# FFN up products as seven block products of eight, on one Trainium2 core

## The chip, the core and the metric

The kernel runs on one core of a Trainium2 chip. Five engines work beside each other, each through its own queue in order: TensorE (PE, matmuls into PSUM; PEld is its weight load), VectorE (DVE), ScalarE (ACT), GpSimd (POOL) and SyncE (SP), which issues the DMAs. The metric is the device time of one execution in microseconds. Less is better.

## The reference

Two layers over 512 latent tokens (x) and 256 context tokens (ctx) of width 1024. Each layer is a half-step SwiGLU FFN, a token mixer (a convolution, gated linear attention and attention beside each other), and a second half-step FFN; each of them is preceded by an RMS norm with a scale, shift and gate that come from a conditioning vector, one set for x and one for ctx.

```python
def pre(x, mod, j, g):
    return rms_norm(x, g) * (1 + mod[:, :, 3 * j + 1]) + mod[:, :, 3 * j]

def half_ffn(x, mod, j, g, w1, w2):
    gu = pre(x, mod, j, g) @ w1
    a, u = jnp.split(gu, 2, axis=-1)
    return x + 0.5 * mod[:, :, 3 * j + 2] * ((jax.nn.silu(a) * u) @ w2)
...
    for i in range(DEPTH):
        mod_x = (sc @ w_ada[i] + b_ada[i]).reshape(B, 1, N_MOD, D)
        mod_c = (scc @ w_ada[i] + b_ada[i]).reshape(1, 1, N_MOD, D)
        x, ctx = layer(x, ctx, mod_x, mod_c, ...)
    return x
```

w1 is 1024 x 5632 (gate and up, 22 tiles of 128 columns each), w2 is 2816 x 1024. In the last FFN only x is needed, so it works on 512 tokens instead of 768.

## The kernel before, in words

Activations lie transposed: 128 channels on the partitions, the 768 tokens along the row (x first), eight K tiles for the width of 1024 (KT = 8). Every product of float32 values is made of three passes: an operand is split into a rounded part and the rest (`split`, lines 141 to 143: a copy on ScalarE, a subtraction on VectorE), and `mm3` (386 to 393) multiplies hi by hi, lo by hi and hi by lo into one PSUM sum. The weights go the same way: `load_split` (132 to 139) loads a tile of 128 x 1024, two load buffers deep, and splits it into `whi` and `wlo`, three deep.

There are four FFNs (two per layer), here called FFN 1 to 4, with a mixer between 1 and 2 and between 3 and 4. `ffn` (402) goes over 22 hidden tiles f. `up` (413) makes the gate tile and the up tile of f: for each of the eight K tiles three passes over two column ranges, 386 and 384 columns (256 and 258 in FFN 4). The columns are the tokens and two more that hold the shifts. The activation that goes in is x times the scale only (class `Scale`, 336): 1 / rms per token comes in when the sum leaves PSUM, in `evac` (462, lines 465 and 468), so products can start before the norm is known. Then silu(gate) times up is split (`gh`, `gl`). `down` (485) multiplies two hidden tiles at a time by w2: for each of eight output tiles d and each of the segments (512 columns of x, 256 of ctx) two times three matmuls, and `add_gated` (line 399, VectorE) adds the sum times the gate onto the residual `xt`. The products of a pair of hidden tiles follow one pair later.

The modulation vectors (w_ada, 1024 x 9216 per layer) are made beside the FFNs: `ada` (183) loads 128 x 512 pieces, ScalarE multiplies them by the conditioning value, once for x and once for ctx (line 195), VectorE adds them up (line 197), and a matmul with a matrix of ones (206) sums over the partitions. `fill` advances them a few steps per hidden tile, so they are spread over the FFN. The first two vectors are made on TensorE at the start (`ada_first`, 211).

`Stats` (247) sums the squares of the finished residual tiles (ScalarE squares, GpSimd adds at line 263), and gets 1 / rms with thirteen small VectorE steps (line 282 and `rsqrt`, 145).

The mixer (`mix`, 518) is a long chain of smaller products. The order of instructions on each engine is set by a planner that weighs costs and due times, with TensorE's order by hand (`tc.manual_schedule`) only in the first products (`up_head`, 429) and in the attention loop. GpSimd has no work in the FFNs but the sums of squares at their ends.

## Time and profile before

| | us |
|---|---|
| median of 3 timed runs | 2857.68 (2856.6 to 2858.29) |
| span of the profiled execution | 2857.3 |
| PE busy | 2781.7 (97%) |
| PEld busy | 2541.2 (89%) |
| DVE busy | 1768.5 (62%) |
| ACT busy | 1200.8 (42%) |
| POOL busy | 136.4 (5%) |

The profiled execution's own time is its span from the first to the last instruction, 2857.3 us; it lies between the timed runs. Busy time of an engine is the time in which at least one of its instructions runs. Matmuls overlap their neighbours by their drain, so the listed duration of one is longer than the step from its start to the next start. A stretch of the span is given as start:end in us; PEclk is the granted TensorE clock as a share of 2.4 GHz.

### The profile page before, as it was taken

Reading aid. Unit: us, or ns where it says so; the run is one execution under the profiler, and the core shown is the slowest. Engines: PE = TensorE matmul, PEld = TensorE weight load, DVE = VectorE, ACT = ScalarE, POOL = GpSimd, SP = SyncE. Lnnn points to the kernel's source line nnn. Section 1 sums busy time; section 2 is a strip of 40 time slices with the busy share of each in tenths; the row PEclk is TensorE's granted clock in tenths of the full one; section 3 lists DMA queues with packets and bytes.
Section 4 is the critical chain, followed back from the end, with each engine's and each line's share of the span. In section 5 each row is a group of like instructions: output and inputs, shape, how many; then the busy total and the mean of one; then the engine's idle time right before and its main releaser. Section 6 shows DMA issues by size and latency. Waiting matters only on the chain. (4 is left out here: it accounts for less than half of the span.)

```text
span 2857.3 us, 42932 instructions
## 1 busy us (share of the span) xinstructions
PE 2781.7 (97%) x17498; PEld 2541.2 (89%) x17498; DVE 1768.5 (62%) x2974; ACT 1200.8 (42%) x1908; POOL 136.4 (5%) x134
## 2 busy tenths in 40 slices
PE   8999999999899999999999999999999989999999
PEld 4999999988687899999999999999997768999998
DVE  4786874464897565566465746454546588555555
ACT  4665662233347454254252523232324447432322
POOL 1000000010300100000000100000001110100000
PEclk9999999999999999999999999999999999999999
DMA  7443441221211243233231313231312131222322
GB/s 255 144 144 129 141 130 60 67 93 58 65 43 27 86 139 101 82 118 107 78 118 56 116 66 111 74 119 60 98 57 84 47 88 28 91 89 95 98 97 89
DMA packets 98501, 267.67 MB, mean 94 GB/s; under 512 B 11520, under 2 KB 11904, under 8 KB 98304
## 3 DMA queue, kind: packets, MB, share of 16 engines
q1 hardware_dynamic: 98304, 264.93, 28.7%
q8 instruction: 137, 2.24, 0.3%
q14 instruction: 60, 0.49, 0.1%
HBM read 249.16 MB, written 7.34 MB: 90 GB/s over the span
## 5 line engine op out<-in xcount | busy, mean ns | idle before, releaser
L137 ACT CAST whi<-raw 128x1024 fp32r<-128x1024 f32 (+1 forms) x314 | 324.6, 1044 | 1110.8 <-PE up L391 524.2
L389 PE MATMUL up<-sh,whi 128*128 128x386 f32 (+1 forms) x2808 | 691.4, 327 | 2.2 <-ACT sh L362 1.2
L391 PE MATMUL up<-sl,whi 128*128 128x386 f32 (+1 forms) x2808 | 687.8, 325 | 4.7 <-DVE sl L363 4.7
L393 PE MATMUL up<-sh,wlo 128*128 128x386 f32 (+1 forms) x2808 | 686.0, 325 | 0.1
L465 DVE TENSOR_TENSOR upv<-up,rb 128x770 f32<-128x770 f32 (+2 forms) x177 | 157.2, 889 | 639.0 <-PE up L393 634.7
L389 PEld LDWEIGHTS up<-sh,whi 128*128 128x128 f32 x2808 | 493.1, 190 | 12.4 <-ACT whi L137 4.2
L391 PEld LDWEIGHTS up<-sl,whi 128*128 128x128 f32 x2808 | 495.9, 190 | 7.5 <-DVE sl L363 7.3
L393 PEld LDWEIGHTS up<-sh,wlo 128*128 128x128 f32 x2808 | 494.1, 190 | 2.1 <-DVE upv L465 1.7
L399 DVE SCALAR_TENSOR_TENSOR xt<-dn,mods,xt 128x512 f32<-128x512 f32 (+1 forms) x616 | 375.2, 632 | 123.0 <-PE dn L393 122.3
L389 PE MATMUL dn<-gh,whi 128*128 128x512 f32 (+1 forms) x1232 | 429.9, 349 | 3.3 <-DVE xt L399 3.2
L138 DVE TENSOR_TENSOR wlo<-raw,whi 128x1024 fp32r<-128x1024 f32 (+1 forms) x314 | 378.6, 1215 | 83.3 <-ACT whi L137 75.1
L391 PE MATMUL dn<-gl,whi 128*128 128x512 f32 (+1 forms) x1232 | 427.7, 347 | 0.0
L393 PE MATMUL dn<-gh,wlo 128*128 128x512 f32 (+1 forms) x1232 | 426.4, 347 | 0.0
L195 ACT ACTIVATE adat<-adaw,sc 128x512 f32<-128x512 f32 x392 | 258.9, 715 | 84.0 <-DVE adacc L197 76.7
L389 PEld LDWEIGHTS dn<-gh,whi 128*128 128x128 f32 x1232 | 232.8, 189 | 45.0 <-ACT whi L137 7.9
L393 PEld LDWEIGHTS dn<-gh,wlo 128*128 128x128 f32 x1232 | 232.9, 189 | 31.2
L391 PEld LDWEIGHTS dn<-gl,whi 128*128 128x128 f32 x1232 | 233.0, 189 | 29.5
L197 DVE TENSOR_TENSOR adacc<-adacc,adat 128x512 f32<-128x512 f32 x392 | 250.4, 684 | 7.9 <-ACT adat L195 6.3
L468 ACT ACTIVATE upv<-upv 128x512 f32<-128x512 f32 (+1 forms) x308 | 179.7, 625 | 33.8 <-DVE upv L465 33.6
L389 PE MATMUL pj<-nh,whi 128*128 128x512 f32 (+1 forms) x328 | 120.5, 371 | 8.5 <-DVE var L572 4.3
L263 POOL TENSOR_TENSOR acc<-acc,sq 128x512 f32<-128x512 f32 (+1 forms) x72 | 76.1, 1057 | 1075.1 <-ACT sq L260 1069.7
L391 PE MATMUL pj<-nl,whi 128*128 128x512 f32 (+1 forms) x328 | 120.9, 369 | 2.4 <-DVE nl L332 2.3
(216 smaller groups left out, 2798.7 us busy)
## 6 DMA issues: line engine op xcount, KB each, us to landing
raw<-in_w_dram SPq DMA_DIRECT2D x264, 512.0 KB, 3.5
adaw<-in_wada_dram SPq DMA_DIRECT2D x288, 256.0 KB, 3.3
raw<-in_wt_dram SPq DMA_DIRECT2D x26, 512.0 KB, 3.4
raw<-in_wo_dram SPq DMA_DIRECT2D x16, 512.0 KB, 3.6
raw<-in_wk_dram SPq DMA_DIRECT2D x8, 416.0 KB, 3.2
xt<-in_xT_dram SPq DMA_DIRECT2D x8, 384.0 KB, 7.9
park<-xt SPq DMA_DIRECT2D x8, 384.0 KB, 2.3
xt<-park SPq DMA_DIRECT2D x8, 384.0 KB, 5.2
```

The source lines that it names most:

```text
L137: nc.scalar.copy(out=hi[:, :n], in_=r[:, :n])
L138: nc.vector.tensor_tensor(out=lo[:, :n], in0=r[:, :n], in1=hi[:, :n].bitcast(F32), op=ALU.subtract)
L195: nc.scalar.activation(out=t, in_=r, func=AF.Copy, scale=sc[:, k, v:v + 1])
L197: nc.vector.tensor_tensor(out=acc[v], in0=acc[v], in1=t, op=ALU.add)
L263: eng.tensor_tensor(out=self.acc[:, t0:t0 + n], in0=self.acc[:, t0:t0 + n], in1=s[:, :n], op=ALU.add)
L389: nc.tensor.matmul(out=o, lhsT=w[0], rhs=m[0][:, t0:t0 + n], start=first, stop=False)
L391: nc.tensor.matmul(out=o, lhsT=w[0], rhs=m[1][:, t0:t0 + n], start=False, stop=False)
L393: nc.tensor.matmul(out=o, lhsT=w[1], rhs=m[0][:, t0:t0 + n], start=False, stop=last)
L399: nc.vector.scalar_tensor_tensor(out=x, in0=o[:, :n], scalar=mods[l][:, v, mod * KT + d:mod * KT + d + 1], in1=x, op0=ALU.mult, op1=ALU.add)
L465: nc.vector.tensor_tensor(out=a[:, t0:t0 + n], in0=p[:, c0:c0 + n], in1=rb[:, t0:t0 + n], op=ALU.mult)
L468: nc.scalar.activation(out=a[:, c], in_=a[:, c], func=AF.Silu if t == f else AF.Identity, bias=a[:, NX + v:NX + v + 1])
```

## The change

The up product of an FFN is a 2 x 2 x 2 block product: the tokens are cut into two halves h (384 each, 256 in FFN 4; half 0 is all x), K into two halves of four K tiles, and the output into gate and up. The Winograd form of Strassen's scheme makes it with seven block products and sums of blocks. In the code they are named by the activation operand: 11 and 21 (half 0, K half 0 and 1), 22 (half 1, K half 1) and T1 to T4 (differences of normalised blocks). Each product is four K tiles times three passes. Partial results are shared: `up` adds products onto PSUM data that ScalarE or VectorE has written (`b` is a copy of `a`, `c` is a sum of `a` and `z`), after one dummy matmul per bank. Four PSUM banks a, b, c, d change roles from one hidden tile to the next.

Since differences of normalised values are needed, the norm is applied before the products (class `Combos` in place of `Scale`): normalise half 0 and split it, then normalise half 1, form the differences (VectorE and GpSimd) and split them. For the first four hidden tiles of an FFN (HEADS) the products 11 and 21, which need half 0 only, come first, while half 1 is being built; their results are kept in SBUF.

The weight operands are sums too: a class `Feed` loads weight tiles (five load buffers), lets GpSimd form the sums of 128 x 512 blocks (four for each hidden tile), and splits them into units of 512 columns, in a ring of seven. A unit is refilled when the product after the one that used it has been issued (`release`). Down products use units of 512 as well, and the last four hidden tiles' down products are made together in `tail`. The mixers' weight tiles become two units each.

In `ffn` all engines' queues now follow the program order (`tc.manual_schedule()` without a list of engines). The modulation vectors advance by `tick`, after each block product and each down tile; per piece VectorE does the product and sum for x in one instruction, ScalarE the product for ctx and GpSimd the sum for ctx. The sum over partitions takes one-column matmuls.

Also changed: the output projection and the last down products of FFN 2 are cut 384 + 384 instead of 512 + 256; the sines and cosines are loaded per mixer.

The diff, cut to its core:

```diff
+HEADS = 4
+RAW = 5
+RING = 7
...
-    def load_split(src, n=1024):
-        r = wp.tile([P, 1024], F32, tag="raw", name="raw", bufs=2)
+    def load(src, n=1024):
+        r = wp.tile([P, 1024], F32, tag="raw", name="raw", bufs=RAW)
         nc.sync.dma_start(out=r[:, :n], in_=src)
-        hi = wp.tile([P, 1024], F32R, tag="whi", name="whi", bufs=3)
-        lo = wp.tile([P, 1024], F32R, tag="wlo", name="wlo", bufs=3)
-        nc.scalar.copy(out=hi[:, :n], in_=r[:, :n])
-        nc.vector.tensor_tensor(out=lo[:, :n], in0=r[:, :n], in1=hi[:, :n].bitcast(F32), op=ALU.subtract)
-        return hi, lo
+        return r
+
+    def unit(src):
+
+        n = src.shape[1]
+        w = wp.tile([P, 2, 512], F32R, tag="w", name="w", bufs=RING)
+        split(w[:, 0, :n], w[:, 1, :n], src)
+        return w[:, 0], w[:, 1]
+
+    def load_split(src, n=512):
+
+        r = load(src, 2 * n)
+        u = [unit(r[:, i * n:(i + 1) * n]) for i in range(2)]
+        return lambda k: tuple(v[:, k % 4 * P:(k % 4 + 1) * P] for v in u[k // 4])
...
+        nxt = fetch(*work[0])
+        yield
+        for i, (m, half, k) in enumerate(work):
+            nv = 1 if l == DEPTH - 1 and m >= 5 else 2
+            r = nxt
+            if i + 1 < len(work):
+                nxt = fetch(*work[i + 1])
+            if k == 0:
+                acc = [slot("q", "adacc", (P, 512)) for v in range(nv)]
+                nc.vector.tensor_scalar(out=acc[0], in0=r, scalar1=sc[:, k, 0:1], scalar2=None, op0=ALU.mult)
+            else:
+                nc.vector.scalar_tensor_tensor(out=acc[0], in0=r, scalar=sc[:, k, 0:1], in1=acc[0],
+                                               op0=ALU.mult, op1=ALU.add)
+            if nv > 1:
+                t = slot("m", "adat", (P, 512)) if k else acc[1]
+                nc.scalar.activation(out=t, in_=r, func=AF.Copy, scale=sc[:, k, 1:2])
+                if k:
+                    nc.gpsimd.tensor_tensor(out=acc[1], in0=acc[1], in1=t, op=ALU.add)
...
+    class Combos(Stats):
...
+        def build(self, h):
+            nh = self.nh
+            yield from self.spread(self.half(h))
+            rb = self.rb
+            for p in range(4):
+                a = self.normed(p, h, rb)
+                if h == 0:
+                    self.h0.append(a)
+                    self.pair("xb", a, self.TAGS["b"], ("11", "21"))
+                else:
+                    t13 = slot("E", "t13", (P, 2, nh))
+                    t24 = slot("E", "t24", (P, 2, nh))
+                    nc.vector.tensor_tensor(out=t13[:, 0], in0=a[:, 0], in1=self.h0[p][:, 0], op=ALU.subtract)
+                    nc.gpsimd.tensor_tensor(out=t24[:, 0], in0=a[:, 1], in1=t13[:, 0], op=ALU.subtract)
+                    nc.vector.tensor_tensor(out=t13[:, 1], in0=a[:, 1], in1=a[:, 0], op=ALU.subtract)
+                    nc.gpsimd.tensor_tensor(out=t24[:, 1], in0=self.h0[p][:, 1], in1=t24[:, 0], op=ALU.subtract)
+                    b = slot(self.TAGS["22"][p], "x22", (P, 2, nh), F32R)
+                    split(b[:, 0], b[:, 1], a[:, 1])
+                    self.x["22"].append((b[:, 0], b[:, 1]))
+                    self.pair("xt", t13, self.TAGS["13"], ("T1", "T3"))
+                    self.pair("xt", t24, self.TAGS["24"], ("T2", "T4"))
+                yield
...
+    class Feed:
...
+            def sums(n):
...
+                ra, ru = staged[n]
+                s1 = slot("v", "s1", (P, 512))
+                pool(s1, ru[:, lo], ru[:, hi], ALU.add)
+                pool(ru[:, lo], ra[:, lo], ru[:, lo])
+                staged[n].append(s1)
+                if order[n][1] < HEADS:
+                    pool(ra[:, lo], s1, ra[:, lo])
+                    pool(ra[:, hi], ra[:, hi], ra[:, lo])
...
+                    plain = fs[0] >= HEADS
+                    if plain:
+                        yield unit(ra[:, lo])
+                        pool(ra[:, lo], s1, ra[:, lo])
+                    yield unit(s1)
+                    yield unit(ra[:, lo])
+                    if plain:
+                        yield unit(ra[:, hi])
+                        pool(ra[:, hi], ra[:, hi], ra[:, lo])
+                    yield unit(ru[:, lo])
+                    sums(n + 1)
+                    yield unit(ra[:, hi])
+                    yield unit(ru[:, hi])
+                else:
+                    if kind == "d":
+                        sums(n + 1)
+                    for c in (lo, hi) if kind != "t" or len(ends_of[l, i]) == 1 else (lo, hi, lo):
+                        for t in r:
+                            yield unit(t[:, c])
...
-        def up(f, uv):
-            for t in (f, FT + f)[len(uv):]:
-                w = load_split(w1_d[l, i, t])
-                p = bigt("up")
-                for k in range(KT):
-                    mm_up([p[:, p0 + t0:p0 + t0 + n] for t0, n in cols], w, k, cols)
-                    if k == FK:
-                        nm.flush()
-                uv.append(evac(f, t, [(p, 0, p0, nt)]))
-            sil, u = uv
-            nc.vector.tensor_tensor(out=sil[:, :nt], in0=u[:, :nt], in1=sil[:, :nt], op=ALU.mult)
-            gh = slot("a" + o, "gh", (P, HW), F32R)
-            gl = slot("b" + o, "gl", (P, HW), F32R)
-            split(gh[:, :nt], gl[:, :nt], sil[:, :nt])
-            return gh, gl
...
+        def release(n):
+            feed.fill(held[0])
+            if feed.free and nxt is not None:
+                nxt.fill(feed.free)
+                feed.free = 0
+            held[0] = n
+
+        def prod(o, b, start):
+            (hi, lo), = feed.get(1)
+            for p in range(4):
+                ws = slice(p * P, (p + 1) * P)
+                for e, (w, m) in enumerate(((hi, b[p][0]), (hi, b[p][1]), (lo, b[p][0]))):
+                    nc.tensor.matmul(out=o, lhsT=w[:, ws], rhs=m, start=start and p == 0 and e == 0,
+                                     stop=p == 3 and e == 2, skip_group_check=True)
+            release(1)
...
+        steps = 2 + 18 * 2 * fill[1]
+        ticks = [0, 0]
+
+        def tick():
+            ticks[0] += 1
+            n = steps * ticks[0] // 230
+            advance(fill[0], n - ticks[1])
+            ticks[1] = n
+
+        def up(f, e, banks):
+            a, b, c, d = banks
+            y = slot("F", "upy", (P, 2, nh))
+            z = slot("F", "upz", (P, 2, nh))
+            if e is None:
+                sa0 = y[:, 0]
+                prod(a, x["11"], True)
+                nc.scalar.copy(out=b, in_=a)
+                tick()
             else:
+                sa0 = e[:, 1]
+                nc.scalar.copy(out=a, in_=e[:, 0])
+            prod(d, x["T1"], True)
+            nc.scalar.copy(out=z[:, 1], in_=d)
+            tick()
+            prod(a, x["T2"], False)
+            add(c, a, z[:, 1])
+            tick()
+            if e is None:
+                prod(b, x["21"], False)
+                silu(sa0, b)
+                tick()
+            prod(a, x["T3"], False)
+            add(z[:, 1], a, z[:, 1])
+            tick()
+            prod(c, x["22"], False)
+            silu(y[:, 1], c)
+            tick()
+            prod(a, x["T4"], False)
+            mul(z[:, 0], sa0, a)
+            mul(z[:, 1], y[:, 1], z[:, 1])
+            t = "E" if f >= FT - 2 else "cEE"[f] + "2" * (f == 0) if f < 3 else ("c2", "d2", "E")[f % 3]
+            gh = slot(t, "gh", (P, 2, nh), F32R)
+            gl = slot(t, "gl", (P, 2, nh), F32R)
+            split(gh, gl, z)
+            tick()
+            return tuple(v.rearrange("p a n -> p (a n)") for v in (gh, gl))
...
+        with tc.manual_schedule():
+            head = {}
+            for f in range(0, HEADS, 2):
+                hs = []
+                for q in range(2):
+                    o = smlt("up", tag="sml")[:, :nh]
+                    e = slot("E" if f < 2 else "d2", "head", (P, 2, nh))
+                    hs.append((o, e))
+                    prod(o, x["11"], True)
+                    nc.scalar.copy(out=e[:, 0], in_=o)
+                    advance(cb.pending)
+                for q, (o, e) in enumerate(hs):
+                    prod(o, x["21"], False)
+                    silu(e[:, 1], o)
+                    head[f + q] = e
+                    advance(cb.pending)
+            advance(cb.pending, KT)
+            t0, t1 = bigt("up"), bigt("up")
+            banks = [t[:, c:c + nh] for t in (t0, t1) for c in (0, 512)]
+            for o in banks:
+                nc.tensor.matmul(out=o, lhsT=x["11"][0][0][:, :P], rhs=x["11"][0][0], start=True, stop=True,
+                                 skip_group_check=True)
+            g = {}
+            for c in range(FT // 2):
+                for q in range(2):
+                    if q == 1 and 0 < c < FT // 2 - 1:
+                        down((g.pop(2 * c - 2), g.pop(2 * c - 1)))
+                    f = 2 * c + q
+                    g[f] = up(f, head.pop(f, None), banks if f % 2 == 0 else [banks[n] for n in (3, 1, 2, 0)])
+            advance(fill[0], 1000)
+            tail([g[f] for f in range(FT - 4, FT)])
```

## Rows read from the trace of the kernel before

**Rows 1.** The page, busy time and its share of the span.

```profile
PE 2781.7 (97%) x17498; PEld 2541.2 (89%) x17498; DVE 1768.5 (62%) x2974; ACT 1200.8 (42%) x1908; POOL 136.4 (5%) x134
```

**Rows 2.** Stretches: start:end, PE, PEld, DVE, ACT, POOL busy, PEclk, DMA, GB/s.

```profile
100.00:617.00 517.00, 517.00 (x2952) 486.54 (x2951) 341.30 (x499) 248.93 (x365) 4.94 (x8) 1.00 0.34 109
...
2475.00:2854.00 379.00, 378.15 (x2677) 354.89 (x2675) 203.88 (x265) 111.02 (x137) 0.99 (x1) 1.00 0.28 93
```

**Rows 3.** Timeline of PE: start, duration, engine, line, operation; x2 merges two.

```profile
129.72 0.51 PE L393 MATMUL up<-sh,wlo 128*128 128x386 f32 x2
...
133.60 0.51 PE L391 MATMUL up<-sl,whi 128*128 128x386 f32 x2
...
601.37 0.40 PE L389 MATMUL dn<-gh,whi 128*128 128x512 f32 x1
...
603.48 0.40 PE L389 MATMUL dn<-gh,whi 128*128 128x512 f32 x1
...
2485.26 0.40 PE L393 MATMUL up<-sh,wlo 128*128 128x256 f32 x2
...
2489.79 0.41 PE L389 MATMUL up<-sh,whi 128*128 128x256 f32 x2
```

**Rows 4.** Groups by line and shape: count, then busy us, mean ns of one.

```profile
L389 PE MATMUL up<-sh,whi 128*128 128x386 f32 x1056 | 361.0, 342 | 2.2 <-ACT sh L362 1.2 <-DVE xt L399 0.9
...
L389 PE MATMUL up<-sh,whi 128*128 128x256 f32 x352 | 99.8, 283 | 0.0
```

**Rows 5.** The same view, instructions of VectorE and ScalarE.

```profile
L138 DVE TENSOR_TENSOR wlo<-raw,whi 128x1024 fp32r<-128x1024 f32 x306 | 370.4, 1220 | 56.0 <-ACT whi L137 50.7
...
L137 ACT CAST whi<-raw 128x1024 fp32r<-128x1024 f32 x306 | 317.5, 1049 | 1086.9 <-PE up L391 524.2 <-PE dn L391 290.5 <-issue 147.0
...
L399 DVE SCALAR_TENSOR_TENSOR xt<-dn,mods,xt 128x512 f32<-128x512 f32 x352 | 261.4, 747 | 120.6 <-PE dn L393 119.9
...
L197 DVE TENSOR_TENSOR adacc<-adacc,adat 128x512 f32<-128x512 f32 x392 | 250.4, 684 | 7.9 <-ACT adat L195 6.3
...
L399 DVE SCALAR_TENSOR_TENSOR xt<-dn,mods,xt 128x256 f32<-128x256 f32 x264 | 125.5, 480 | 2.4 <-PE dn L393 2.4
...
L143 DVE TENSOR_TENSOR gl<-upv,gh 128x770 fp32r<-128x770 f32 x66 | 63.1, 957 | 25.7 <-ACT gh L142 25.5
...
L976 ACT COPY pt<-tp 128x384 f32<-128x384 f32 x64 | 30.2, 472 | 18.8 <-PE tp L972 18.1
```

**Rows 6.** The same view, the sums of GpSimd.

```profile
L263 POOL TENSOR_TENSOR acc<-acc,sq 128x512 f32<-128x512 f32 x30 | 40.0, 1334 | 197.5 <-ACT sq L260 193.6 <-DVE nrm L328 3.4
...
L263 POOL TENSOR_TENSOR acc<-acc,sq 128x256 f32<-128x256 f32 x42 | 36.1, 860 | 877.6 <-ACT sq L260 876.1
```

**Rows 7.** A stretch around the change from FFN 2 to FFN 3.

```profile
1565.00:1605.00 40.00, 36.99 (x196) 32.33 (x194) 37.14 (x63) 26.59 (x47) 13.75 (x12) 0.91 0.29 91
```

**Rows 8.** Timeline of VectorE, the last nine of the thirteen steps: first and last.

```profile
639.31 0.15 DVE L155 TENSOR_TENSOR rsq_a<-rsq_y 128x4 f32<-128x4 f32 x1
...
640.88 0.16 DVE L157 SCALAR_TENSOR_TENSOR rsq_y<-rsq_a,rsq_y 128x4 f32<-128x4 f32 x1
```

**Rows 9.** Evacuations of up products: ns min/median/max, first and last start us.

```profile
L465 DVE TENSOR_TENSOR upv<-up,rb x177: 550/960/964, 72.4 to 2831.4; 128x770 f32<-128x770 f32 x131, 128x514 f32<-128x514 f32 x44, 128x386 f32<-128x386 f32 x1, 128x384 f32<-128x384 f32 x1
```

**Rows 10.** Timeline of GpSimd and VectorE near the start of the kernel.

```profile
26.20 2.05 POOL L263 TENSOR_TENSOR acc<-acc,sq 128x512 f32<-128x512 f32 x1 [0.16 <-ACT sq L260]
27.04 1.76 DVE L363 SCALAR_TENSOR_TENSOR sl<-xt,gs,sh 128x512 fp32r<-128x512 f32 x1
...
29.75 1.28 POOL L263 TENSOR_TENSOR acc<-acc,sq 128x512 f32<-128x512 f32 x1 [1.50 <-ACT sq L260]
29.78 1.54 DVE L363 SCALAR_TENSOR_TENSOR sl<-xt,gs,sh 128x256 fp32r<-128x256 f32 x1
```

582 lines of the change are left out of this document (255 added, 327 removed).

## Prediction

> **What bounds the kernel now.** I read the totals first, then stretches, then single engines. TensorE is busy 97% of the span [rows 1]; by stretches it is 517.00 of 517.00 us inside the first FFN, 378.15 of 379.00 in the last [rows 2], so inside the FFNs nothing but its own matmuls counts. The profiled span is 2857.3 us; the three timed runs are 2856.6 to 2858.3, so the sum is made against 2857.3 and carried over unchanged. What a matmul costs there is the step from one start to the next, not its listed duration (neighbours overlap): eleven pairs of up products of 386 and 384 columns take 3.88 us, 0.176 us each; nineteen pairs of 256 and 258 take 4.53 us, 0.119 us each; one output tile of the down product, 12 matmuls, takes 2.11 us [rows 3].
>
> **What the change removes.** A hidden tile f (gate and up) now takes 2 weight tiles x 8 K tiles x 3 passes x 2 column ranges = 96 matmuls; the counts agree (1056 = 22 x 2 x 8 x 3 FFNs per pass and range [rows 4]). Seven products of 4 K tiles x 3 passes are 84, of 384 columns (256 in the last FFN). In three FFNs that saves 12 x 0.176 = 2.1 us per tile and 0.03 us for the two shift columns, 2.15 x 66 = 142 us; in the last 12 x 0.119 and the same trifle, 1.47 x 22 = 32 us. Together **-174.5 us**. Down products, projections and attention keep their matmuls; the output projection is cut 384+384 instead of 512+256, the same 768 columns. The modulation vectors' sums go from wide to one-column matmuls, of which I take the balance as nothing, within 5 us either way. So 2683 us is the floor; the rest is what the new arrangement makes TensorE wait for.
>
> **The engines' share.** For a pair of tiles TensorE now needs 2 x 14.8 + 8 x 2.11 = 46.4 us. VectorE has 18 weight splits of 512 columns (half of 1.22, say 0.65 with the start of an instruction), 16 residual updates (8 x 0.747 + 8 x 0.480), six combinations with an operand in PSUM (0.61 between the 256 and 512 rows), two products and two splits of 768 (0.96): 11.7 + 9.8 + 3.7 + 1 + 1.9 = 28 us [rows 5]. ScalarE's copies (0.52 and 0.47) come to less. GpSimd, idle in the FFNs before, gets eight weight sums of 1.33 us [rows 6], 10.6 us. By shares all fit under 46.4. The cover of the handovers inside a tile is one product, 2.1 us: the copy b<-a runs beside T1, the sum c beside the 21 product, the second sum beside 22.
>
> **Where the cover is missing (heads).** The first four tiles of each FFN have products 11 and 21 done earlier, so T3 follows T2 at once and overwrites what VectorE must read first; and T1 of tiles 1 and 2 overwrites the bank of the T4 just ended. Each such turn costs the drain (0.34 shown less the step of 0.176), one 384-column VectorE instruction (0.61) and about 0.1 for signals: 0.88 us [rows 3 to 5]. Six per FFN, 24 in all: **+21 us**; ends 12 (the drain apart) and 32 (a split queued in front).
>
> **Where the cover is missing (FFN starts).** Before, x times g went in raw and 1/rms followed at the evacuation, so up products began at once: around the second start (1565 to 1605) TensorE is busy 36.99 of 40 us, at a mean granted clock of 0.91 [rows 7]. Now half 0 must be normalised before the heads, half 1 and its four differences before T1. After the last x tile come square and sums, then thirteen small VectorE steps 0.2 us apart [rows 8], then transposes: about 6 us. Then per K pair VectorE has four normalising steps (1.6), two differences (1.1), three splits (0.55 + 2 x 0.96) and a unit and a half for the ring (1.0): 6.2 us, and waits for two GpSimd differences of about 1.1 us in its chain: 7.5 us. Four make 30; T1 can start some 3 us before the last ends, so 33 us after the residual. The heads cover 8 x 2.11 = 17 us, plus 1 for the transposes. TensorE idles 15 us and pays about 2 more for the clock: in [rows 7] three idle us went with 9% of 40 us of clock, so some 7 us at 1.2 GHz. With the 2 us a start that was lost before (5, 0 and 1) taken off, three starts (FFN 2 to 4): **+45 us**; ends 20 (GpSimd and splits out of the chain) and 65. At the kernel's start the first evacuation was at 72.4 us, with three of 44 weight tiles, 25 us, done by about 77 [rows 9]; now the heads' 17 us are done and T1 starts at about 73 to 79: **+5 us**, ends -3 and +12.
>
> **The modulation vectors.** Their steps are spread as (2 + 36 m) x tick / 230, while only 1 + 18 m steps exist: they are used up at tick 115 of 218, so they fill the first half of an FFN. In FFN 1 (m = 7) that is 24 steps a pair: 21 VectorE instructions of about 0.7 and 19 GpSimd sums of 1.33. VectorE (28 and 15) then has 43 us of 46.4, GpSimd (10.6 and 25) 36. They don't run beside each other: while GpSimd's sum ran from 26.20 to 28.25, VectorE's 512-column instruction of 0.75 took 1.76 us, and a 256-column one 1.54 us beside the sum that started at 29.75 [rows 10]. The instructions with both inputs in SBUF (splits, modulation) are 28 of VectorE's 43; with GpSimd's 35 that is 63, less 0.14 us at each of 27 handovers, 59 us a pair against 46.4. Over 5.2 pairs: +66 if all of it shows, 0 if none. I take **+40**: the rows lie at the upper end, but seven units of ring (15 us) and VectorE being the late one at the start anyway (10 us) pay part once. FFN 2 (m = 5): 16 steps, 50 against 46.4, +0 to +19, **+6**; FFN 3 makes four vectors for x only, without GpSimd sums; FFN 4 none.
>
> The Trainium skill ("SBUF — State Buffer", section "Who interferes with whom") says that a VectorE instruction with two SBUF inputs and a GpSimd instruction that reads SBUF exclude each other for the whole instruction, whoever issues first. The 1.76 and 1.54 us above agree; by the page without the handovers' gain the term would be +86 instead of +66 at its upper end. The rule speaks against the weight sums on GpSimd everywhere; the sum above does not need it.
>
> **Mixers.** A weight tile costs two splits of 512 instead of one of 1024, about 0.1 us more on VectorE for 50 tiles, against a deeper ring and five load buffers: **+2**, ends -10 and +10, since the planner sets the order there anew.
>
> Sum: -174.5 + 21 + 45 + 5 + 40 + 6 + 2 = -55.5, so **2802 us**.
>
> **The rivals.**
> (a) The covers hold: GpSimd's sums fall into VectorE's PSUM work, differences are ready earlier. All lower ends: -174.5 + 12 + 20 - 3 + 5 - 5 = -145, **2712 us**, reaching to 2760. For: VectorE's share outside modulation is only 28 of 46.4. Against: [rows 10].
> (b) Slower: the turn inside a product. VectorE and ScalarE take instructions in order; if a split that waits for GpSimd (1.3 us) stands before the sum c, the cover of 2.1 us is used up: 0.65 + 1.3 + 0.61 + 0.3 = 2.9 us, 0.8 late, once or twice a tile. At 1 us on each of 84 tiles it is +84, **2886 us**; it decides from 0.6 us per tile on (50 us over 84 tiles). For: in modulation stretches VectorE has hardly any slack. Against: only four GpSimd sums per seven products, and 8.4 us of down products per tile in which VectorE catches up.
> (c) It doesn't do what it says: two banks each share one PSUM tile, and if waits are set by tile and not by bank, each product waits for the neighbour's handover: 7 x 0.88 x 88 = +542 us, **3344 us**. No row shows such a pair.
>
> **Chances.** About 0.2% is what a measurement here can tell from no change, 2852 to 2863. Forecast (2760 to 2850) 0.50; (a) 0.27; (b) 0.18; (c) 0.02; remainder between, 0.03. Faster 0.77, same 0.04, slower 0.19. The range 2730 to 2865 leaves out the better part of (a) (0.10) and of (b) (0.10); the forecast's own is 2760 to 2850.
>
> **What would show it.** Up matmuls 7392 of 384 and 256 columns at 0.176 and 0.119 us. Idle TensorE at T1 of each FFN's first tile, 15 us, released by the splits of the differences (DVE). Waits of T3 on the sum c in tiles 0 to 3, 0.9 us. A first half of FFN 1 longer per pair than its second half (54 against 46.4 us), with VectorE's splits at 1 to 1.9 us there. Wrong if the pairs are equal (then (a)), if late products stand in all tiles ((b)), or if the mixers' stretches differ by more than 10 us.

## The result, and the profile after

The changed kernel takes 3296.89 us (3295.35 to 3298.47) where the kernel before takes 2857.98: a ratio of 1.153, with an interval from 1.152 to 1.155. The forecast was 2802 us, so the time moved by 439 us in the other direction. The profiled execution has a span of 3296.4 us.

The page of the changed kernel, its busy line; the answer to [rows 1]:

```profile
PE 2863.3 (87%) x16890; PEld 2578.4 (78%) x16890; DVE 2160.9 (66%) x3579; ACT 1248.3 (38%) x2330; POOL 935.1 (28%) x686
```

TensorE went from 97% busy to 87%, and GpSimd from 5% to 28%. To see where the time went, I read one event that both kernels have once per hidden tile, ScalarE's rounding copy of the product of gate and up. Timeline of ScalarE (start, duration, engine, line, operation), of the kernel before, first and last tile of FFN 1:

```profile
80.88 0.82 ACT L142 CAST gh<-upv 128x770 fp32r<-128x770 f32 x1
...
594.69 0.84 ACT L142 CAST gh<-upv 128x770 fp32r<-128x770 f32 x1 [1.53 <-DVE upv L423]
```

The same of the changed kernel:

```profile
131.76 0.83 ACT L143 CAST gh<-upz 128x768 fp32r<-128x768 f32 x1 [2.36 <-DVE upz L539]
...
758.96 0.83 ACT L143 CAST gh<-upz 128x768 fp32r<-128x768 f32 x1 [2.99 <-DVE upz L539]
```

With the same two lines of FFN 2, 3 and 4, the difference after less before, piece by piece (us):

| piece | before | after | difference |
|---|---|---|---|
| kernel's start to first tile | 80.9 | 131.8 | +50.9 |
| FFN 1, first to last tile | 513.8 | 627.2 | +113.4 |
| to FFN 2's first tile (tail, mixer 1, start) | 442.6 | 500.3 | +57.7 |
| FFN 2 | 516.4 | 595.6 | +79.2 |
| to FFN 3's first tile (tail, start) | 63.5 | 111.0 | +47.5 |
| FFN 3 | 513.3 | 521.9 | +8.6 |
| to FFN 4's first tile (tail, mixer 2, start) | 363.6 | 410.5 | +46.9 |
| FFN 4 | 339.9 | 373.1 | +33.2 |
| end | | | +1.8 |

In these rows "tail" means the last down products of an FFN, and "start" the time from there, or from the mixer's end, to the next FFN's first finished tile. Thirteen products now stand before a first tile is done (13 x 12 x 0.1735 = 27.1 us) instead of 96 matmuls (16.9), so 10 us of each "to" row, and of the kernel's start, are moved work, 7 in FFN 4; what the starts and mixers lost is the rest, some 41, 47, 37 and 40 us. And every FFN lost inside, where I had forecast a gain.

Windows of the changed kernel (start:end, length, busy time of PE, PEld, DVE, ACT, POOL, granted clock, DMA share, GB/s): the stretch of [rows 2], 50 us from the first half of FFN 1, 50 us from its second, and the start of FFN 2:

```profile
100.00:617.00 517.00, 423.38 (x2149) 388.19 (x2150) 376.82 (x499) 196.85 (x339) 243.39 (x166) 0.88 0.31 104
350.00:400.00 50.00, 39.69 (x193) 36.45 (x192) 36.63 (x45) 19.06 (x33) 24.62 (x17) 0.83 0.34 116
650.00:700.00 50.00, 46.42 (x260) 42.84 (x259) 28.41 (x44) 15.40 (x28) 11.37 (x8) 1.00 0.19 64
1195.00:1250.00 55.00, 34.16 (x133) 30.03 (x133) 47.83 (x72) 31.64 (x61) 27.02 (x19) 0.72 0.16 53
```

Three kinds of loss show. In the quiet second half (no modulation steps) TensorE is at its full clock and still misses 3.6 of 50 us; a pair of tiles ("quiet pair" below) takes 50.9 us instead of the 46.4 worked out. In the first half it misses 10 us, the granted clock is 0.83, and a pair takes 67 to 82. At the FFN's start it misses 21 of 55, at 0.72, while VectorE is busy 48.

TensorE's idle time in a quiet pair (timeline, the rows from 600 to 655 us that have any):

```profile
607.62 0.45 PE L534 MATMUL up<-xth,w 128*128 128x384 f32 x1 [0.55 <-ACT up L557]
...
616.89 2.38 PE L534 MATMUL up<-x,w 128*128 128x384 f32 x12 [0.65 <-DVE upz L538]
...
619.85 0.44 PE L534 MATMUL up<-xth,w 128*128 128x384 f32 x1 [0.58 <-ACT upy L540]
...
629.65 0.45 PE L534 MATMUL up<-xbh,w 128*128 128x384 f32 x1 [1.22 <-DVE up L538]
...
632.59 0.44 PE L534 MATMUL up<-xth,w 128*128 128x384 f32 x1 [0.58 <-ACT upy L540]
```

Take the last row. Product T3 writes bank a; it waits for silu (line 540), which reads bank b. No data passes between them, and a and b are two halves of one PSUM tile (in an even tile f; in an odd one the banks go 3, 1, 2, 0, so there a and c share one, and b and d). All five rows are of that kind: T1 into d waits for the copy that writes b; 22 into c waits for the sum that reads a, and T4 into a for the silu that reads c; 21 into b waits for the sum that reads a. That is what rival (c) describes; e1 below tests it.

Groups of instructions of the changed kernel (count, busy us, mean ns of one, idle time before), VectorE and GpSimd; the answers to [rows 5, 6]:

```profile
L144 DVE TENSOR_TENSOR w<-raw,w 128x512 fp32r<-128x512 f32 x800 | 690.3, 879 | 367.2 <-ACT w L143 355.3
...
L202 POOL TENSOR_TENSOR adacc<-adacc,adat 128x512 f32<-128x512 f32 x168 | 245.5, 1461 | 289.9 <-ACT adat L200 257.2 <-issue 21.4 <-PE up L534 9.6
...
L196 DVE SCALAR_TENSOR_TENSOR adacc<-adaw,sc,adacc 128x512 f32<-128x512 f32 x224 | 241.4, 1078 | 2.4 <-DMA adaw<-in_wada_dram 2.1
```

A 512-column split was 0.65 us in my sum and takes 879 ns in the mean; the modulation sum, which I put at about 0.7, takes 1078.

TensorE's waits over the whole changed kernel (who waited for whom: us in total, times, longest), the first five:

```profile
PE up L534 <- DVE up L538: 101.7, 53, 7.9
PE up L534 <- ACT upy L540: 42.0, 76, 0.6
PE up L534 <- DVE upz L538: 35.6, 42, 3.4
PE up L534 <- ACT head L630: 27.1, 7, 7.0
PE adaps L208 <- DVE adacc L196: 26.3, 10, 6.9
```

### The profile page after: what moved, and what is told of

It is laid out like the page before. It is cut to its first block, busy times and chain, and to the rows that moved or that the text cites. A ratio compares the mean times of both kernels' runs of the same rounds, so it can differ in the third digit from the quotient of the medians.

```text
span 3296.4 us, 43983 instructions
## 1 busy us (share of the span) xinstructions
PE 2863.3 (87%) x16890; PEld 2578.4 (78%) x16890; DVE 2160.9 (66%) x3579; ACT 1248.3 (38%) x2330; POOL 935.1 (28%) x686
## 4 chain that ended last, share of the span: by engine, by line
PE 61%; DVE 17%; ACT 10%; issue 6%; POOL 5%; DMA 1%; SPq 0%; POOLq 0%; DVEq 0%; ACTq 0%
PE up L534 28%; DVE w L144 5%; PE dn L411 5%; PE dn L413 5%; PE dn L415 5%; POOL adacc L202 2%; DVE upz L539 2%; DVE adacc L196 2%; PE pj L411 2%; ACT w L143 2%; DVE xt L422 2%; PE adaps L230 2%; PE pj L413 2%; PE pj L415 2%; PE adaps L208 2%
## 5 line engine op out<-in xcount | busy, mean ns | idle before, releaser
L144 DVE TENSOR_TENSOR w<-raw,w 128x512 fp32r<-128x512 f32 (+1 forms) x816 | 699.6, 873 | 393.7 <-ACT w L143 381.8
L534 PE MATMUL up<-xth,w 128*128 128x384 f32 (+1 forms) x2816 | 749.3, 337 | 112.3 <-ACT upy L540 42.0
L143 ACT CAST w<-raw 128x512 fp32r<-128x512 f32 (+1 forms) x816 | 493.2, 615 | 659.2 <-PE dn L415 341.2
L534 PEld LDWEIGHTS up<-xth,w 128*128 128x128 f32 x2816 | 519.0, 196 | 156.8 <-ACT upy L540 65.9
L534 PE MATMUL up<-xbh,w 128*128 128x384 f32 (+1 forms) x1408 | 403.7, 355 | 137.7 <-DVE up L538 68.8
L534 PE MATMUL up<-xtl,w 128*128 128x384 f32 (+1 forms) x1408 | 466.3, 331 | 3.0 <-DVE xtl L144 3.0
L411 PE MATMUL dn<-gh,w 128*128 128x512 f32 (+2 forms) x1232 | 440.8, 358 | 18.4 <-DVE xt L422 14.5
L422 DVE SCALAR_TENSOR_TENSOR xt<-dn,mods,xt 128x512 f32<-128x512 f32 (+3 forms) x568 | 341.2, 625 | 151.0 <-PE dn L415 149.6
L415 PE MATMUL dn<-gh,w 128*128 128x512 f32 (+2 forms) x1232 | 432.9, 351 | 3.4 <-DVE w L144 3.4
L413 PE MATMUL dn<-gl,w 128*128 128x512 f32 (+2 forms) x1232 | 434.2, 352 | 1.8 <-DVE gl L144 1.8
L534 PEld LDWEIGHTS up<-xbh,w 128*128 128x128 f32 x1408 | 280.3, 210 | 156.5 <-DVE up L538 79.2
L411 PEld LDWEIGHTS dn<-gh,w 128*128 128x128 f32 x1232 | 240.0, 195 | 60.5 <-DVE xt L422 24.7
L415 PEld LDWEIGHTS dn<-gh,w 128*128 128x128 f32 x1232 | 238.6, 194 | 35.0 <-DVE w L144 5.4
```

Source lines behind the costliest of these rows:

```text
L143: nc.scalar.copy(out=hi, in_=src)
L144: nc.vector.tensor_tensor(out=lo, in0=src, in1=hi.bitcast(F32), op=ALU.subtract)
L411: nc.tensor.matmul(out=o, lhsT=w[0], rhs=m[0][:, t0:t0 + n], start=first, stop=False)
L413: nc.tensor.matmul(out=o, lhsT=w[0], rhs=m[1][:, t0:t0 + n], start=False, stop=False)
L415: nc.tensor.matmul(out=o, lhsT=w[1], rhs=m[0][:, t0:t0 + n], start=False, stop=last)
L422: nc.vector.scalar_tensor_tensor(out=x, in0=o[:, a - t0:b - t0], scalar=mods[l][:, v, mod * KT + d:mod * KT + d + 1], in1=x, op0=ALU.mult, ...
```

## The experiments

All are the changed kernel with one or more edits, each timed once; the code shown is the core of the edit. "Pair" is the time from one first tile of a pair to the next, read from the same ScalarE copies. The kernel before took 2857.6 to 2861.7 us beside them, so I read nothing into differences below 5 us.

**e1_banks: one PSUM tile per bank.**

```diff
-            t0, t1 = bigt("up"), bigt("up")
-            banks = [t[:, c:c + nh] for t in (t0, t1) for c in (0, 512)]
+            psum_as("quad", 1)
+            banks = [wide[0].tile([P, 512], F32, tag=f"q{i}", name="up")[:, :nh] for i in range(4)]
```

> The four accumulators of the up products become four PSUM tiles of one bank each instead of halves of two tiles; nothing else changes. Theory A (waits are set per tile: a product that writes one half waits until the engine that reads the other half has ended): the quiet second half of FFN 1 goes from 50.9 us per pair of tiles to 46.4-47.5, and the whole kernel loses 110 to 170 us (3130 to 3190), less (80) if the first halves stay bound by VectorE and GpSimd. Theory B (VectorE and ScalarE are late because of what stands in their queues before the handover): quiet pairs stay at 50 to 51 us and the time falls by less than 40.

(`psum_as` is a helper that opens another set of PSUM tiles; behind the hidden tiles the two-bank tiles come back.)

Measured: 3139.2 us, 158 less. Quiet pairs take 45.9 us, and the same two windows read:

```profile
350.00:400.00 50.00, 39.47 (x189) 37.25 (x188) 37.60 (x42) 20.18 (x35) 25.22 (x17) 0.84 0.32 111
650.00:700.00 50.00, 50.00 (x289) 47.94 (x288) 31.31 (x47) 16.96 (x32) 11.95 (x9) 1.00 0.21 70
```

In the quiet window TensorE no longer waits at all, with all the engines' work unchanged, so the five waits are shown to come from the shared tile (theory A). The window with modulation steps did not move: the five full pairs of FFN 1 that have such steps take 367 us together in both kernels, so there it gained nothing to take these waits away. The Trainium skill ("PSUM — Partial Sum Buffer", section "🎯 Summary: rules for kernel authors") tells authors to read another bank than the one a matmul writes, and to guard by bank. In both kernels the reads are of another bank; in the changed kernel the guard went by a tile of two banks, and that cost the 158 us.

**e2_even: the modulation steps over the whole FFN.** The pace is `min(old, max(20, (18 * m + 2) * tick // 205))`, with m vectors.

> The same modulation steps, but after the first vector (which the first down product needs) spread over the whole FFN instead of its first half. In the changed kernel the modulation steps come to some 1.0 us of extra time each (124 us for 126 steps in FFN 1, 90 us for 90 in FFN 2). Theory A (VectorE and GpSimd, which shut each other out, are full in the first half and have room in the second): FFN 1 loses 50 to 80 us, FFN 2 40 to 60, the whole 90 to 140. Theory B (each step costs TensorE the same wherever it stands, since TensorE itself waits for the sums and runs their matmuls): 0, within 25.

Measured: 3225.3 us, 72 less, between the two. FFN 1 lost 41 us and FFN 2 29. Its pairs now take 53 to 69 us all along. The seven pairs of FFN 1 with about twelve modulation sums of VectorE each take 60.6 us in the mean, 9.7 over the quiet 50.9 or 0.8 us a sum; the changed kernel's four pairs with 19 to 22 sums take 73.9, 1.1 us a sum. So there is room in the second half, but this pace doesn't make the steps free.

**e3_vadd: the second sum on VectorE.**

```diff
-                    nc.gpsimd.tensor_tensor(out=acc[1], in0=acc[1], in1=t, op=ALU.add)
+                    nc.vector.tensor_tensor(out=acc[1], in0=acc[1], in1=t, op=ALU.add)
```

> The second modulation sum is added on VectorE instead of GpSimd. Theory A (the exclusion between the two engines is what the modulation steps cost): VectorE gets 216 instructions of about 0.75 us, but no longer waits while GpSimd's 1.46 us sums run; the first halves of FFN 1 and 2 fall from about 74 to 60-64 us per pair, the whole by 80 to 150. Theory B (VectorE's own work is the bound there): slower, by up to 216 x 0.75 = 160 us.

Measured: 3270.8 us, 26 less: neither. (The moved additions are 168, not 216.) GpSimd's busy time between 200 and 450 us fell from 130 to 44 us, but VectorE's stayed at 188 (190 in the changed kernel). Its sum and its splits there take 840 and 703 ns in the mean:

```profile
L196 DVE SCALAR_TENSOR_TENSOR adacc<-adaw,sc,adacc 128x512 f32<-128x512 f32 x63 | 52.9, 840 | 0.8 <-DMA adaw<-in_wada_dram 0.7
...
L144 DVE TENSOR_TENSOR w<-raw,w 128x512 fp32r<-128x512 f32 x55 | 38.2, 703 | 8.5 <-ACT w L143 8.5
```

In the changed kernel they take 1143 and 1156. VectorE's instructions did get shorter, and its 63 additions (801 ns, 50.5 us) took the place of what that freed. So the exclusion shows, but taking it away while the work stays was worth only 26 us.

**e4_pemod: the steps on TensorE.** `nc.tensor.matmul(out=ps[:nv, :], lhsT=sc[:, k, :nv], rhs=r, start=k == 0, stop=k == KT - 1)` takes the place of the sums; pieces are loaded three ahead, ScalarE copies each finished half vector, four small transposes follow, and the down products use one PSUM bank less.

> The modulation sums inside the FFNs are taken off VectorE, GpSimd and ScalarE altogether: TensorE multiplies each loaded 128x512 fp32 tile with the two conditioning columns as weights and sums over K in PSUM (one matmul per step; before it, eight matmuls of one column per eight steps). The pace stays that of the first half. Theory A (those engines' time and exclusion): a modulated pair of tiles falls from about 74 us to 50.9 + 24 x 0.25 = 57, FFN 3 by some 10, the whole by 130 to 190 us. Theory B (TensorE's own part of the steps, or their loads): the pairs stay above 68 and the whole falls by less than 60.

Measured: 3322.5 us, 26 more. My price for the step was wrong: in the timeline the next product starts 0.95 us after this matmul, where I had put 0.25. Its group, and then the window 200 to 450 us (where the changed kernel has 200.34 us of PE at a clock of 0.87):

```profile
L194 PE MATMUL adaps<-adaw,sc 128*2 128x512 f32 (+1 forms) x512 | 258.2, 591 | 1.7 <-PE adaps L201 1.0 <-PE up L527 0.7
```

```profile
200.00:450.00 250.00, 246.83 (x1107) 163.82 (x1107) 100.33 (x178) 60.46 (x110) 38.06 (x28) 1.00 0.38 126
```

As a test of the cause it still tells something: with the steps off the other engines TensorE waits 3 of 250 us and keeps its full clock. The time gained there went back into its own matmuls, 256 x 0.95 = 243 us. The edit isn't clean: quiet pairs take 53.3 us here instead of 50.9, with one PSUM bank less.

**e5_banks_nomod: e1 without the modulation steps.** `ada` returns at once.

> On the kernel with four one-bank tiles (3139.2 us) all modulation steps inside the FFNs are left out: their loads, sums and matmuls, so the later modulation vectors are constants (0.1, and 0.5 for the scales). The rest runs as before. Theory A (the longer first halves are the modulation steps and nothing else): FFN 1, 2 and 3, which took 602.6, 553.4 and 474.5 us from their first to their last tile, take 456 to 460 each, so the whole falls by about 258 us to 2881 (2865 to 2900), and what is left of the loss against the kernel before stands at the FFN starts. Theory B (part of the first halves is something else, for instance waits of the ring of weights): they stay above 475 and the whole above 2930.

Measured: 2859.6 us, 280 less than e1. FFN 1, 2 and 3 take 449.8, 449.8 and 449.6 us and every full pair 45.9: theory A, even a little below its range. So with two causes gone, and without the modulation work that the kernel before does, the changed kernel only just equals it. What is left against it stands before the first tiles (134.4, 502.2, 108.7 and 409.6 us there) and in FFN 4, which takes 328.6 us and had 339.9 in the kernel before.

**e6_banks_lag: three empty steps ahead of the one-column matmuls**, on e1.

> On the kernel with four one-bank tiles (3139.2 us): three empty steps stand between a modulation vector's last sum and the one-column matmuls that read it; the pace is raised so that the steps still end at half of the FFN. Theory A (TensorE runs in order and stands at these matmuls until VectorE's queue has come to the sum, 30.9 us of the 250 between 200 and 450 us): these waits fall below 8 us there and the whole loses 35 to 60 us. Theory B (VectorE and GpSimd are simply full there): the idle time moves to the up and down products, and the whole changes by less than 15 us.

Measured: 3105.5 us, 34 less. TensorE's waits between 200 and 450 us, of e1 and then of this run, the first four each:

```profile
PE adaps L217 <- DVE adacc L205: 30.9, 7, 8.1
PE up L543 <- DVE up L547: 6.4, 2, 3.6
PE dn L420 <- DVE xt L431: 5.0, 3, 4.5
PE up L543 <- DVE upz L547: 1.2, 1, 1.2
```

```profile
PE up L545 <- DVE up L549: 16.0, 5, 4.9
PE dn L422 <- DVE xt L433: 12.6, 6, 5.8
PE up L545 <- ACT up L568: 5.8, 3, 2.7
PE up L545 <- DVE upz L550: 4.1, 1, 4.1
```

The wait of the vector's matmuls for the sum fell from 30.9 to 1.8 us, and nearly all of it comes back in this stretch as waits of the up and down products for VectorE and, 5.8 us of them, ScalarE (from 12.6 us in e1's rows to 38.5 in the first four here). So the order costs something, 34 us (A said 35 to 60), but in this stretch the place is mostly where a late VectorE shows first: between A and B.

**e7_banks_first: the first two vectors as before**, on e1 (32-column weights, 512 columns, transposes).

> On the kernel with four one-bank tiles (3139.2 us): the first two modulation vectors are again summed as in the kernel before (32 columns of weights, 512 columns per matmul, then transposes: 32 wide matmuls instead of 128 pairs of 2 columns). Theory A (TensorE's 54.9 us of 2-column matmuls delay the kernel's start): the first tile is done 15 to 25 us earlier than at 133.5 us, and the whole loses as much. Theory B (VectorE's and ScalarE's building of the normalised halves sets the start): 0, within 5.

Measured: 3118.7 us, 20 less; the first tile is done at 112.5 us instead of 133.5. Theory A. The groups of one- and two-column matmuls in the changed kernel: first the one for all later vectors, then the one at the kernel's start that this edit takes away:

```profile
L208 PE MATMUL adaps<-glb,adacc 128*128 128x1 f32 x448 | 69.6, 282 | 47.2 <-DVE adacc L196 26.3 <-DVE xt L422 19.1 <-POOL adacc L202 1.1
...
L230 PE MATMUL adaps<-sc,adaw 128*128 128x2 f32 x256 | 54.9, 352 | 6.0 <-DMA adaw<-in_wada_dram 6.0
```

**e8_combined: e1, e3, e7, the lag of e6 and an even pace together.**

> Five edits together: one-bank tiles, the old form of the first two vectors, the second modulation sum on VectorE, the steps spread over the whole FFN, and three empty steps ahead of the one-column matmuls. Theory A (each relieves something of its own): 3139 - 26 - 72 - 45 - 20 = 2976 us (2950 to 3000). Theory B (the middle three relieve the same thing, VectorE's full queue): 3030 to 3060.

Measured: 2980.7 us. The effects add up (2976 expected; 2987 with the 34 us that e6 measured), and FFN 1, 2 and 3 take 532.6, 503.2 and 465.0 us. It is the fastest but one of the runs that compute the whole, and still 4% slower than the kernel before.

**e9_chain, e10_chain_pc, e11_chain_pc_ring: the order at the FFN starts**, on e8. First `advance(self.pending)` right behind the last square of the second half; then also `PC = [1, 1, 1, 1, 1, 1, 0, 0]`; then also `nxt.fill(3)` two tiles before the end of FFN 2's down product.

> On the combined kernel (2980.7 us): when the last x tile of the second half is done, the sums of squares and the thirteen small VectorE steps of 1/rms are issued at once, ahead of the weight splits that refill the ring (seven in a row, 4.30 us, at the start of FFN 3) and of GpSimd's weight sums (beside which some of the thirteen steps take 1.1 us instead of 0.16). Theory A (what stands in VectorE's queue before the chain is part of the lost start): each of the starts of FFN 2 to 4 gets 4 to 9 us shorter, the whole 12 to 27. Theory B (the building of the second half, 7 us per pair on VectorE, sets the start and follows on whatever comes): within 5 us.

> As the run with the early chain, and the normalising steps of the first half are spread over the first six x tiles of the second instead of up to the last. Theory A (the heads wait for the first half's last operands, whose building ends only after the last x tile): heads start up to 5 us earlier, the whole loses 0 to 15 us more. Theory B (the heads wait for their weights, which come after it all): within 5 us.

> As the run before it, and three of the seven weight units for the heads of the next FFN are split during the last two output tiles of FFN 2's down product instead of after them (only the start of FFN 3). Theory A (the 10.3 us that TensorE stands there before the first head are the ring's refill): the start of FFN 3 gets 5 to 9 us shorter. Theory B (T1 waits for the second half's building anyway, so that heads that start earlier only wait later): less than 2 us.

Measured: 2986.9, 2986.0 and 2992.1 us. The start of FFN 3 goes from 109.0 to 106.3, 105.9 and 106.5 us, the stretch before FFN 2's first tile from 500.0 to 498.6, 497.9 and 498.8; other pieces lose as much or more, so that e9 is 6 us slower than e8 where theory B allowed 5. The gain of theory A shows in none of them: these three orders of the small work are not what sets the starts.

**e12_chain_build: the eight differences of GpSimd on VectorE**, on e9.

> As the run with the early chain; the eight GpSimd differences in the building of the second half go to VectorE (8 x 0.56 us more on it). Theory A (VectorE's work sets the starts: building takes four times 7.1 us of its time): the four starts get 0 to 4 us longer each. Theory B (the chain through GpSimd's 1.2 to 1.4 us differences and their exclusion sets it): 3 to 8 us shorter each, 12 to 30 for the whole.

Measured: 2977.1 us, 10 less than e9; the four stretches before first tiles get 1.6, 3.1, 0.9 and 4.4 us shorter (1.5 of the last lie in mixer 2). The handover to GpSimd cost a little more than the work it took, less than theory B said.

**e13_banks_nosum2: e1 without GpSimd's modulation sums.**

> On the kernel with four one-bank tiles (3139.2 us) GpSimd's 196 additions of the second modulation sum are left out, so that this sum holds its first term only; ScalarE's products, VectorE's sum and all matmuls stay. Theory A (the exclusion: beside these sums VectorE's 512-column sum takes 1204 ns instead of 0.74 us and its splits 1148 instead of 0.69, and ScalarE stands 45 of 250 us behind them): both go back to under 0.85 us, the first halves of FFN 1 and 2 fall to 50 to 56 us per pair, the whole by 110 to 170 us. Theory B (VectorE's own modulation work and TensorE's in-order waits are the larger part): by 30 to 80 us.

Measured: 3000.9 us, 138 less than e1: theory A in the whole, though pairs of FFN 1 still take 56 to 63 us. (The sums left out are 168, as in the row of line 202 above, not 196.) The two VectorE groups between 200 and 450 us, of e1 and then of this run:

```profile
L205 DVE SCALAR_TENSOR_TENSOR adacc<-adaw,sc,adacc 128x512 f32<-128x512 f32 x61 | 73.5, 1204 | 0.8 <-DMA adaw<-in_wada_dram 0.5
...
L153 DVE TENSOR_TENSOR w<-raw,w 128x512 fp32r<-128x512 f32 x54 | 61.5, 1148 | 17.5 <-ACT w L152 16.8
```

```profile
L205 DVE SCALAR_TENSOR_TENSOR adacc<-adaw,sc,adacc 128x512 f32<-128x512 f32 x77 | 67.3, 874 | 5.7 <-DMA adaw<-in_wada_dram 5.4
...
L153 DVE TENSOR_TENSOR w<-raw,w 128x512 fp32r<-128x512 f32 x64 | 46.3, 734 | 14.0 <-ACT w L152 13.8
```

The same instructions on the same data sizes take 330 and 414 ns less once the neighbour is quieter (its weight sums stay). GpSimd's sums are thus half of what the modulation steps cost (138 of 280 us). The Trainium skill ("SBUF — State Buffer", section "Who interferes with whom") says that the two engines exclude each other for whole instructions; these means agree with it. The 138 us are the price of the sums as a whole, exclusion and work together: e3, which took away the first and kept the second (with the shared PSUM tiles), gained 26.

**e14_alias: less to build at the starts**, on e8. T2, T4 and 22 use the operands of T1, T3 and 21.

> On the combined kernel (2980.7 us): products T2, T4 and 22 use the operands of T1, T3 and 21, so that in the building of the second half two of the four differences (GpSimd's), their split and the split of x22 are left out; the products stay. Per pair of K tiles VectorE has 2.7 us of 7.1 less, GpSimd 2.5. Theory A (VectorE's building of the second half sets when T1 can start): T1 of each FFN comes 10 to 14 us earlier, the whole falls by 40 to 56 us. Theory B (the chain sums, 1/rms, heads on TensorE and ScalarE sets it): by less than 12.

Measured: 2950.8 us, 30 less, below theory A's range for the whole. The stretches before the first tiles of FFN 1, 2 and 3 get 10.5, 13.1 and 11.7 us shorter, as theory A says; that of FFN 4 only 1.9 (4.7 from the mixer's end on, with a mixer 2.7 us longer). FFN 2 takes 6.2 us more inside, for which I have no reason shown. The edit leaves out VectorE's splits and GpSimd's differences together, so it doesn't tell the two apart.

## Why the prediction was wrong, point by point

The saved matmuls were priced rightly; the waits were not. The step that failed is the one from engine shares to "what the new arrangement makes TensorE wait for": the wait for a neighbour in the same PSUM tile was left out of the sum (158 us measured), the modulation steps were put at 46 us and cost 280, and the FFN starts were put at 50 and cost some 140.

**The matmuls were right, the gain was there in three of the four FFNs.** There are 7392 up matmuls, and an undisturbed step of 384 columns is 0.1735 us. With one-bank tiles and no modulation (e5) FFN 1 takes 449.8 us from first to last tile; 141 products of 12 x 0.1735 and nine pairs' down products of 16.9 make 446. So the 142 us of the first three FFNs were there to be had. The 32 us of FFN 4 were not: the same working gives some 300 us for its 256 columns, and e5 takes 328.6 where the kernel before took 339.9. Its first ten products behind the first tile take 22.8 us instead of 14.3 (TensorE busy 18.0, clock 0.93), and its later pairs 32.6 instead of some 31.

**The heads were right in FFN 1 to 3.** From an FFN's first tile to its third, e5 takes 25.4 us for ten products (20.8), and to its fifth another 42.4 for twelve products and a pair's down products (41.9): 5 us an FFN, which makes 20 in all, as forecast (21), if FFN 4's 5 are counted like the others'.

**Rival (c) was right as a mechanism; its price and its chance were wrong.** It got 0.02 with the words "No row shows such a pair". That no row of before shows a mechanism is no evidence against it: before, the two halves of an up tile were filled and evacuated together (one evacuation of 770 columns, [rows 9]), so no row could. The price assumed a wait at each of seven products; only five per pair have a neighbour at work at that moment, at about 1 us each (0.55 to 1.22 idle and the refill), so it was 158 us (e1), not 542. That its total of 3344 us lies near the measured 3297 is luck: most of the difference came from elsewhere. As a term of the sum instead of a rival it would have taken nearly all of the gain by itself.

**The modulation steps: +46 forecast, 280 measured (e5 against e1).** Four parts failed. (1) The balance of the matmuls, taken as nothing within 5 us: a half vector's sixteen one-column records take 1.71 us at the full clock (3.4 us for a vector), where the kernel before needed eight records of 1.0 us together and four transposes of 0.35 us together; over the sixteen vectors that is some 26 us more. The 2-column form at the kernel's start costs another 20 (e7); these stand in the start's 41 below, not in the 280. (2) GpSimd's sums: I had set an upper end of 66 us for the exclusion in FFN 1 and taken 40, counting on slack; the sums are worth 138 (e13). I had left out that they also hold up ScalarE: in e1 its products wait 45.1 of 250 us for slots that GpSimd still reads, a wait that e13 doesn't have. (The wait of VectorE's splits for ScalarE's copies hardly changes, 16.8 us in e1 and 13.8 in e13.) How the 138 divide between this and the exclusion isn't shown. (3) I compared engine shares with 46.4 us a pair, as if the work could be placed freely; TensorE, in order, stands at late sums (e6), and with twelve sums a pair a sum still costs 0.8 us (e2). (4) No term held the clock in the modulated half. The window from 200 to 450 us, of e1 and of e5:

```profile
200.00:450.00 250.00, 204.59 (x1020) 191.64 (x1020) 191.30 (x237) 96.61 (x164) 129.18 (x87) 0.84 0.34 115
```

```profile
200.00:450.00 250.00, 250.00 (x1438) 237.60 (x1438) 161.61 (x245) 81.15 (x148) 60.20 (x43) 1.00 0.19 64
```

In e1 TensorE is idle for 45 us; the 1020 matmuls that it runs, each at its step in the quiet stretches (0.1735 us for 384 columns, other widths in proportion, 0.107 for one column), would take some 167 us and take 205. So by this estimate some 37 us more went into matmuls at the granted clock of 0.84, nearly as much as the waits. What the other 142 us of the steps divide into, beyond TensorE's matmuls (448 records, 1.71 us for sixteen: 48 us), is not settled.

**The FFN starts: +50 forecast, some 140 measured** (41 at the kernel's start; 34, 37 and 28 at the later ones, when the mixers' part is taken off). The start of FFN 3 in the changed kernel shows it; VectorE's timeline from the last residual to T1:

```profile
1899.17 0.74 DVE L422 SCALAR_TENSOR_TENSOR xt<-dn,mods,xt 128x128 f32<-128x128 f32 x2
...
1903.37 4.30 DVE L144 TENSOR_TENSOR w<-raw,w 128x512 fp32r<-128x512 f32 x7
1910.07 0.16 DVE L282 TENSOR_SCALAR var<-st 128x3 f32<-128x3 f32 x1 [2.40 <-PE st L279]
1910.26 1.27 DVE L150 TENSOR_SCALAR rsq_y<-var 128x3 int32<-128x3 int32 x1
...
1911.77 1.12 DVE L156 TENSOR_TENSOR rsq_a<-rsq_y 128x3 f32<-128x3 f32 x1
1912.93 0.16 DVE L157 TENSOR_TENSOR rsq_a<-rsq_a,rsq_n 128x3 f32<-128x3 f32 x1
...
1916.55 1.38 DVE L378 SCALAR_TENSOR_TENSOR h<-xt,gs,st 128x128 f32<-128x128 f32 x4
...
1926.45 1.38 DVE L378 SCALAR_TENSOR_TENSOR h<-xt,gs,st 128x128 f32<-128x128 f32 x4
...
1933.51 1.38 DVE L378 SCALAR_TENSOR_TENSOR h<-xt,gs,st 128x128 f32<-128x128 f32 x4
...
1942.57 1.38 DVE L378 SCALAR_TENSOR_TENSOR h<-xt,gs,st 128x128 f32<-128x128 f32 x4
```

The four building steps are 7.1 to 9.9 us apart, 8.7 in the mean (7.5 forecast). What I left out stands ahead of them: the last of half 0's own operands (3.6 us), a refill of seven weight units (4.30) and a wait for the sums; the first step starts 17 us after the residual, not 6, and T1 stands at 1944.5, 45 us behind it, not 33. The other failing is the cover. TensorE's idle rows there:

```profile
1903.04 0.69 PE L534 MATMUL up<-xbh,w 128*128 128x384 f32 x1 [10.29 <-ACT w L143]
...
1925.90 0.44 PE L534 MATMUL up<-xbh,w 128*128 128x384 f32 x1 [2.04 <-ACT head L540]
...
1932.95 0.44 PE L534 MATMUL up<-xbh,w 128*128 128x384 f32 x1 [3.48 <-ACT head L630]
...
1940.02 0.45 PE L534 MATMUL up<-xbh,w 128*128 128x384 f32 x1 [3.31 <-ACT head L630]
```

The window over the whole of it, the answer to [rows 7]:

```profile
1892.00:1944.00 52.00, 31.00 (x118) 28.48 (x116) 41.24 (x70) 27.70 (x54) 20.30 (x16) 0.70 0.12 41
```

The heads are 17 us of work, but TensorE waits 10.3 us for their weights first, then between them for ScalarE's copies behind the building, and the granted clock of the stretch is 0.70. Of 52 us it is idle 21; its matmuls, some 18 us at the full step, take the other 31, so the clock cost some 13 us here (estimate) where I had charged 2. Moving the small steps about gained nothing in the whole (e9 to e11), taking work out of the building shortened the starts by 5 to 13 us (e14). So the building of the second half, VectorE's splits and GpSimd's differences, is part of what sets the start; the rest of the 140 us is located, but not tried.

**The mixers: +2 forecast.** From the last tile of FFN 1 to the last output projection 434.8 us instead of 421.1, and 360.6 instead of 348.8 in mixer 2: +26 in all, above the 10 us that I had named as the mark. The cause was not tried.

**A sum of the prediction.** Rival (a) says "all lower ends", but its sum does not take them: with 0 for the modulation steps and -10 for the mixers it is -155.5, not -145. Nothing in the outcome hangs on it.

Together: -174.5 + 20 + 158 + (280 less the 22 that the kernel before spent on its own modulation matmuls) + 140 + 26 = 428 of 439 us. The pieces depend on the order in which they were taken away (the 280 were measured with the banks already apart, and the 158 left the modulated pairs as they were), and what FFN 4 lost beyond its heads, some 20 us, is in none of them. So they give the sizes, not an exact division.

## What to carry to other kernels

When an accumulator is handed between TensorE and other engines, list for every product which other instruction touches the same tile (and not only the same bank) at that moment, and put the wait into the sum even if no old trace can show it. Work that goes to an engine with spare time must be priced at what it does to the queues of its neighbours: here half of a 280 us loss came from sums on an engine that had been 5% busy. And give the clock a term of its own: in the stretches with long waits here it cost nearly as much as the waits. Before matmuls are saved by preparing operands, read what lies between the last input and the first product at each phase's start; 28 to 41 us at each of four starts were enough to eat most of what the saved matmuls would have given.

## What the runs showed of the hardware that I had not expected

- A 512-column fp32 matmul with two columns of weights holds TensorE for 0.95 us (two records, e4). In the kernel before, four matmuls of 32 weight columns each, written to different 32-partition groups, took 1.0 us together (eight records, the first four of which start within 0.02 us, as at 226.95 us): they ran beside each other.
- Of VectorE's smallest steps, 128x3 elements and mostly 0.15 to 0.17 us each, three took 1.12 to 1.27 us where GpSimd's four weight sums of 1.26 to 1.29 us ran beside them (from 1908.89 to 1914.23 us). Each of the three ended within 0.02 us of the end of such a sum (1911.53, 1912.89 and 1914.24 us, the sums at 1911.51, 1912.88 and 1914.23). The steps between them, and all after the last sum, took their 0.15 to 0.17.
- The granted clock was 0.83 in the modulated half of FFN 1, 0.70 at the start of FFN 3, where TensorE stood idle for 10.3, 1.8, 2.0, 3.5 and 3.3 us, and 1.00 in the quiet half with its waits of 0.55 to 1.22 us. At FFN 3's start the matmuls of 384 columns start 0.32 us apart behind the first of these waits (1905.24 to 1907.16 us) and 0.175 apart from 1919.85 to 1923.52 us: the levels of 1.2 and 2.4 GHz.
